# Attention scores of both maps as 64-row matmuls in the two halves of the array, three products each instead of four

## The chip, the cores and the metric

The kernel runs on one core of one Trainium2 chip. The metric is the device time of one execution in microseconds. Before the change the median of three runs is 3787.49 us (3784.84 to 3788.64).

## What is computed

One encoder block on 2048 tokens of 1024 channels: RMS norm, a projection, differential attention, a Hyena branch with long convolutions, the gated merge of both branches, and an expert-choice feed-forward layer with 16 experts. The change touches the differential attention alone: 4 heads, and for each head two softmax maps (m = 0 and 1) over queries and keys of 64 columns.

```python
def diff_attention(q, k, v, lam, subln_g, lambda_init):
    ...
    def block(qi):
        s = jnp.einsum('bhmqd,bhmkd->bhmqk', qi, k).astype(jnp.float32) * scale
        pr = jax.nn.softmax(s, axis=-1)
        a = pr[:, :, 0] - lam * pr[:, :, 1]
        return jnp.einsum('bhqk,bhkd->bhqd', a.astype(v.dtype), v)
    ...
```

## The kernel before

Numbers are carried as two parts, hi and lo, of 12 significant bits each, since the matmuls read the type float32r. A product a·b of two such numbers is taken as hi·hi + hi·lo + lo·hi (`mm3`, three matmuls, L48 to L50); the `split` of a tile is a copy on ACT (L42) and a subtraction on DVE (L43).

The program runs through five stages: the projection, the attention with pieces of the gate projection between its steps, the Hyena branch, the merge, and the experts. The change lies in `attn_phase` (L301). Its work is cut into 32 units, one for each head and each block of 256 queries. A unit has eight score steps, eight turns and eight steps of values:

- `prep_k` (L327) loads the keys of a head, splits them and transposes them, 512 tokens at a time, into the tile `k2`. The hi and the lo part of one map lie stacked in the 128 partitions: hi in partitions 0 to 63, lo in 64 to 127.
- `prep_q` (L355) does the same for the 256 queries of a unit, but writes each part twice: [hi; hi] and [lo; lo]. It takes 8 transposes (L367) and two copies on ACT (L368) a unit.
- `scores` (L388) is called eight times a unit. Each call takes one map, 128 queries and 1024 keys, in two pieces of 512 keys. A piece is two matmuls (L410) of 128 rows and 512 columns into one PSUM tile `p`: [hi; hi] and then [lo; lo] against [hi; lo] of the keys, which makes all four products. DVE then scales the piece into the tile `x` and takes its maximum (L411). After the second call of a map, ACT takes the exponentials of its 2048 columns (L418).
- `combine` (L420) puts the two maps of 128 queries together on DVE; `turn` (L429) transposes the result (L433) and splits it; `values` (L440) multiplies it with v (`mm3` into `pv`). The turns run 11 steps and the values 13 steps behind the scores.
- 150 pieces of `gate_steps` (L253), six matmuls of 512 columns into `gp` each, run between the steps.

The order in which the instructions stand on each engine is not that of the code: the tile framework schedules them when the kernel is built, and the engine then takes them in that order. Two pools that matter for it are these:

```python
        px = ctx.enter_context(pool_of(tc, name="at_s", bufs=6))
        ...
        ss = ctx.enter_context(pool_of(tc, name="at_ps", bufs=3, space=PSUM))
```

`at_ps` holds the PSUM tiles `p` of the scores, three of them, one bank each; `at_s` holds the tiles `x`.

Of the kernel before, what the change touches and what calls it, by code (L numbers as in the profile page):

```python
# [19 lines left out]
L = 2048  # L20
# [57 lines left out]
def rsqrt(nc, dst, tmp, src):  # L78
    """dst = src ** -0.5 with one Newton step after the activation table's root; src is kept."""
# [8 lines left out]
def rsqrt_mean(nc, dst, tmp, ss, n):  # L88
    """dst = (ss / n + EPS) ** -0.5; ss is overwritten."""
# [4 lines left out]
def proj_phase(E, x, norm1_g, w_in, conv_w, conv_b, qg, kg, rope, qn, kn, vs, hyc, ud, sg, mlp, gen):  # L94
    """u = RMSNorm(x); u @ w_in; q and k normed and turned, hy convolved; u turned, in two parts, to ud.
    The first 512 gate columns go to sg as gate_steps makes the others: they are last, token by token, for their
    u leaves its place to what follows.

    mlp and gen make generators of small pieces of other work, run between the products."""
    nc, tc = E.nc, E.tc  # L100
    with ExitStack() as ctx:
# [56 lines left out]
        def turned(c, w, t, pq):  # L158
            """q (c = 0) or k (c = 1): normed per 64 columns, with the rotation of the first 16."""
# [141 lines left out]
def attn_phase(E, qn, kn, vs, lams, subln_g, oT, filler, pieces):  # L301
    """Differential attention; oT [512 channels, tokens] gets the normed output.

    So many pieces of the filler run between its steps, for the vector engine holds the attention."""
    nc, tc = E.nc, E.tc
    QB = 256
    with ExitStack() as ctx:
# [19 lines left out]
        def prep_k(h, b):  # L327
            """k per map, [hi; lo] stacked along the contraction."""
            if b == 0:
                K2[h] = pk.tile([128, 2, L], F32R, name="k2")  # L330
            r = pr.tile([128, 4, 2, DK], F32, name="r")
            i = (nc.sync if h else nc.gpsimd).dma_start(r, dap(kn, b * 512 * 512 + h * 128, [[512, 128], [128 * 512, 4], [DK, 2],
                                                                                    [1, DK]]))
            if h == 0 and b == 1:
                E.second_k = i
            s = pr.tile([128, 4, 2, 2, DK], F32R, name="s")
            if h:
                split(nc, s[:, :, :, 0], s[:, :, :, 1], r)
            else:
                nc.vector.tensor_copy(s[:, :, :, 0], r)  # L340
                nc.vector.tensor_tensor(s[:, :, :, 1], r, s[:, :, :, 0].bitcast(F32), ALU.subtract)
            for m in range(2):
                p = sp.tile([128, 512], F32R, name="pp")
                for j in range(4):
                    nc.tensor.transpose(p[:, j * 128:(j + 1) * 128], s[:, j, m].rearrange("p a d -> p (a d)"), idr)
                nc.scalar.activation(K2[h][:, m, b * 512:(b + 1) * 512], p.bitcast(F32), AF.Copy)
# [8 lines left out]
        def prep_q(h, qb):  # L355
            """The queries of each map: [hi; hi] and [lo; lo] along the contraction."""
            r = pq.tile([128, 4, DK], F32, name="qr")
            nc.sync.dma_start(r.rearrange("p (t m) d -> p t (m d)", t=2),
                              dap(qn, qb * 256 * 512 + h * 128, [[512, 128], [128 * 512, 2], [1, 128]]))
            hl = pq.tile([128, 4, 2, 2, DK], F32R, name="qhl")  # L360
            r2 = r[:, :, None, :].to_broadcast([128, 4, 2, DK])
            split(nc, hl[:, :, 0], hl[:, :, 1], r2)
            qT = pq.tile([128, 4, 2, 128], F32R, name="qT")
            for a in range(2):
                p = sp.tile([128, 4, 128], F32R, name="pp")
                for tm in range(4):
                    nc.tensor.transpose(p[:, tm], hl[:, tm, a].rearrange("p a d -> p (a d)"), idr)  # L367
                nc.scalar.activation(qT[:, :, a], p.bitcast(F32), AF.Copy)  # L368
# [19 lines left out]
        def scores(u, c8):  # L388
            """One of eight steps: 1024 keys of one map for 128 queries; then the exponentials."""
            h, qb = units[u]  # L390
            t, m, c = c8 // 4, (c8 // 2) % 2, c8 % 2
# [8 lines left out]
            if m == 0 and c == 0:  # L400
                SM[u, t] = pq.tile([128, 12], F32, name="sm", bufs=6)
            sm = SM[u, t]
            if c == 0:
                EX[u, t, m] = px.tile([128, L], F32, name="x")
            x = EX[u, t, m]
            for i in range(2):
                o = c * 1024 + i * 512
                p = ss.tile([128, 512], F32, name="p")
                for a in range(2):
                    nc.tensor.matmul(p, qT[:, t * 2 + m, a], k2[:, m, o:o + 512], start=a == 0, stop=a == 1)  # L410
                nc.vector.tensor_scalar(x[:, o:o + 512], p, 0.125, None, ALU.mult, ALU.max,  # L411
                                        accum_out=sm[:, c * 2 + i:c * 2 + i + 1])
            if c == 0:
                return
            nc.vector.tensor_scalar(sm[:, 4:8], sm[:, 0:4], -1.0, None, ALU.mult, ALU.min,  # L415
                                    accum_out=sm[:, 8 + m:9 + m])
            acc = s0[:, qi:qi + 1] if m == 0 else sm[:, 10:11]
            nc.scalar.activation(x, x, AF.Exp, bias=sm[:, 8 + m:9 + m], accum_out=acc)  # L418
# [96 lines left out]
def hyena_tables():  # L515
    """Tables that hang on the shapes alone: positions, decay, and the pieces of a 4096-point DFT."""
# [33 lines left out]
    def parts(a):  # L550
        """The 12 significant bits that float32r carries, and the next 12."""
# [20 lines left out]
def filter_mlp(E, w, tabs, hsd):  # L572
    """The sine MLP on the positions; hsd gets the last layer as [hi; lo] along its channels.

    A generator: each step is a small piece of work, to run between another phase's."""
    nc, tc = E.nc, E.tc
    with pool_of(tc, name="fl_m", bufs=1, side="right") as pm, pool_of(tc, name="fl_ps", bufs=2, space=PSUM) as ps:
# [17 lines left out]
        def sine(p, out, layer):  # L595
            """out = sin(freq * (p + b)) with the argument brought into [-pi, pi] first."""
# [32 lines left out]
def filter_gen(E, w, tabs, hsd, filt):  # L629
    """filt [o, even/odd] (channel, t): sum and difference of the two sides of the filters, in steps."""  # L630
# [38 lines left out]
def hyena_phase(E, hyc, filt, skip, tabs, scr, hT, filler, then):  # L669
    """Two rounds of z <- gate * (conv(z) + skip * z) with 4096-point DFTs on the tensor engine.  # L670

    n = n2 + 128 n1 and k = k1 + 32 k2: first over n1 (16 of 32 are not zero), then, per k1, over n2 with the
    twiddles in the matrix; k1 from 0 to 16 is enough, since all sequences are real. What is left of
    the filler runs between the first steps; then(steps) runs the last steps between its own."""
    nc, tc = E.nc, E.tc
    vscr, z1 = scr["v"], scr["z1"]
    with pool_of(tc, name="hy_d", bufs=1) as pd, ExitStack() as right:
        with ExitStack() as ctx:
# [10 lines left out]
            def sums(v):  # L689
                """The factors of the sums over n1, with the imaginary ones negated for v = 1."""  # L690
# [32 lines left out]
            def parts_of(jobs):  # L723
                """The operands of the sums over n1, in their two parts: loads run ahead, and so does the split."""
# [28 lines left out]
            def first(it, v, side, busy=False):  # L753
                """B[n2, kr, c]: the sums over n1, in their two parts."""
# [17 lines left out]
            def dft_part(p, B, k, cr, ci):  # L772
                """cr times the real and ci times the imaginary sums over n1, over n2, for k1 = k."""
# [11 lines left out]
            def spectrum(it, s, side, busy=False):  # L785
                """The filter's spectrum: the real part (s = 0) and the imaginary one, negated (s = 1)."""
# [69 lines left out]
            def last(o, hf):  # L856
                """Back to n = n2 + 128 n1 with the sums over k1; then the skip and the gate."""
# [82 lines left out]
def merge_phase(E, x, sg, oT, hT, w_pa, w_ph, w_o, norm2_g, w_router, out, u2d, kept, steps):  # L940
    """x1 = x + (gates * branches) @ w_o to out, its norm to u2d, and the router's softmax into E.aff [128, tile, 16]
    of a pool that kept closes.

    steps: the last of the phase before, which makes hT; the first products of the attention branch run between."""
    nc, tc = E.nc, E.tc
    LEAD, AT = 3, (4, 10, 20, 26)
    with ExitStack() as ctx:
# [24 lines left out]
        def load(n, t):  # L972
            """The tile's branch and its gates."""
# [603 lines left out]
```

## Time and profile before

| what | before |
|---|---|
| median of 3 runs | 3787.49 us |
| lowest and highest run | 3784.84 and 3788.64 us |
| span of the profiled execution (its own time) | 3779.5 us |
| instructions in it | 58391 |
| PE busy | 3628.1 us, 96% of the span |
| DVE busy | 2399.3 us, 63% |
| ACT busy | 1739.1 us, 46% |
| mean granted TensorE clock | 0.980 |

The span is counted from the first to the last instruction; no time of that execution other than its span is shown, and the median of the runs is 8.0 us longer than it. In the rows below PE is the matmul part of TensorE and PEld its load of weights. A matmul's time in a row includes the tail in which its last columns leave the array, which lies beside the next matmul; the time that it takes from the engine is the distance from its start to the start of the next one.

### The profile page before, as it was taken

Reading aid. Unit: us, or ns where it says so; the run is one execution under the profiler, and the core shown is the slowest. Engines: PE = TensorE matmul, PEld = TensorE weight load, DVE = VectorE, ACT = ScalarE, POOL = GpSimd, SP = SyncE. Lnnn points to the kernel's source line nnn. Section 1 sums busy time; section 2 is a strip of 40 time slices with the busy share of each in tenths; the row PEclk is TensorE's granted clock in tenths of the full one; section 3 lists DMA queues with packets and bytes.
Section 4 is the critical chain, followed back from the end, with each engine's and each line's share of the span. In section 5 each row is a group of like instructions: output and inputs, shape, how many; then the busy total and the mean of one; then the engine's idle time right before and its main releaser. Section 6 shows DMA issues by size and latency. Waiting matters only on the chain. (4 is left out here: it accounts for less than half of the span.)

```text
span 3779.5 us, 58391 instructions
## 1 busy us (share of the span) xinstructions
PE 3628.1 (96%) x22727; PEld 3214.9 (85%) x22727; DVE 2399.3 (63%) x5111; ACT 1739.1 (46%) x2577; POOL 487.7 (13%) x436
## 2 busy tenths in 40 slices
PE   8999999999999999999999799995999999999998
PEld 6788888788888888799998588885889999999997
DVE  8944552698889897177778543447875555555553
ACT  5411111566666675367766433332344444444443
POOL 0000000000000000354454000003330101101000
PEclk9999999999999999999999799996999999999999
DMA  4286774323222232766776743333556666666664
GB/s 157 76 255 161 190 188 122 114 63 101 83 73 92 65 96 73 229 192 213 234 218 208 250 154 115 128 109 123 167 179 204 219 201 206 217 201 207 217 201 123
DMA packets 448681, 607.43 MB, mean 161 GB/s; under 512 B 36427, under 2 KB 332371, under 8 KB 441749
## 3 DMA queue, kind: packets, MB, share of 16 engines
q1 hardware_dynamic: 388261, 438.80, 36.7%
q0 software_dynamic: 34736, 127.16, 12.3%
q10 hardware_dynamic: 25408, 37.76, 2.8%
q8 instruction: 178, 2.92, 0.3%
q14 instruction: 98, 0.80, 0.1%
HBM read 464.16 MB, written 139.46 MB: 160 GB/s over the span
## 5 line engine op out<-in xcount | busy, mean ns | idle before, releaser
L43 DVE TENSOR_TENSOR wl<-r,wh 128x2048 fp32r<-128x2048 f32 (+1 forms) x232 | 440.7, 1904 | 336.4 <-ACT wh L42 336.1
L42 ACT ACTIVATE wh<-r 128x2048 fp32r<-128x2048 f32 (+1 forms) x232 | 372.1, 1605 | 567.4 <-issue 225.2
L48 PE MATMUL pg<-xh,wh 128*128 128x256 f32 x2048 | 584.4, 285 | 0.0
L49 PE MATMUL pg<-xl,wh 128*128 128x256 f32 x2048 | 581.2, 284 | 0.0
L50 PE MATMUL pg<-xh,wl 128*128 128x256 f32 x2048 | 581.0, 284 | 0.0
L48 PEld LDWEIGHTS pg<-xh,wh 128*128 128x128 f32 x2048 | 394.9, 193 | 5.9 <-ACT s L1461 5.3
L49 PEld LDWEIGHTS pg<-xl,wh 128*128 128x128 f32 x2048 | 394.9, 193 | 0.5
L50 PEld LDWEIGHTS pg<-xh,wl 128*128 128x128 f32 x2048 | 394.7, 193 | 0.0
L411 DVE TENSOR_SCALAR_CACHE_REDUCE x<-p 128x512 f32<-128x512 f32 x512 | 335.3, 686 | 25.0 <-PE p L410 24.2
L410 PE MATMUL p<-k,qT 128*128 128x512 f32 x1024 | 327.4, 415 | 0.0
L418 ACT ACTIVATE x<-x,sm 128x2048 f32<-128x2048 f32 x128 | 256.7, 2006 | 45.8 <-DVE sm L415 42.2
L42 ACT ACTIVATE ah<-pt 128x512 fp32r<-128x512 f32 x256 | 150.2, 595 | 153.4 <-PE pt L433 152.9
L48 PE MATMUL py<-wh,hh 128*128 128x512 f32 x512 | 205.0, 400 | 0.0
L48 PE MATMUL p<-wh,uh 128*128 128x512 f32 x512 | 203.6, 398 | 0.4 <-ACT uh L134 0.4
L49 PE MATMUL py<-wl,hh 128*128 128x512 f32 x512 | 202.8, 396 | 0.0
L50 PE MATMUL py<-wh,hl 128*128 128x512 f32 x512 | 202.8, 396 | 0.0
L50 PE MATMUL p<-wh,ul 128*128 128x512 f32 x512 | 200.4, 392 | 0.0
L49 PE MATMUL p<-wl,uh 128*128 128x512 f32 x512 | 200.3, 392 | 0.0
L43 DVE TENSOR_TENSOR al<-pt,ah 128x512 fp32r<-128x512 f32 x256 | 175.1, 686 | 38.6 <-ACT ah L42 37.3
L43 DVE TENSOR_TENSOR bl<-p,bh 128x512 fp32r<-128x512 f32 x192 | 124.8, 686 | 114.2 <-ACT bh L42 113.2
L410 PEld LDWEIGHTS p<-k,qT 128*128 128x128 f32 x1024 | 171.5, 190 | 24.5 <-ACT qT L368 2.8
L1484 POOL DMA_INDIRECT out_dram<-y,ix x32 | 68.5, 2141 | 778.8 <-ACT y L1483 672.2
(391 smaller groups left out, 9311.2 us busy)
## 6 DMA issues: line engine op xcount, KB each, us to landing
r<-in_w_gate SPq DMA_DIRECT2D x64, 1024.0 KB, 5.1
r<-in_w_up SPq DMA_DIRECT2D x64, 1024.0 KB
r<-in_w_down SPq DMA_DIRECT2D x64, 1024.0 KB, 5.8
gu<-s_ud POOLq DMA_DIRECT2D x48, 1024.0 KB, 5.9
tg<-in_tg POOLq DMA_DIRECT2D x68, 384.0 KB, 4.1
xt<-in_x SPq DMA_DIRECT2D x32, 512.0 KB, 6.5
s_filt<-fo SPq DMA_DIRECT2D x128, 128.0 KB, 3.2
zr<-s_filt SPq DMA_DIRECT2D x64, 256.0 KB, 2.7
```

The costliest lines, as they stand in the source:

```text
L42: nc.scalar.activation(hi, src, AF.Copy)
L43: nc.vector.tensor_tensor(lo, src, hi.bitcast(F32), ALU.subtract)
L48: nc.tensor.matmul(out, a[0], b[0], start=start, stop=False)
L49: nc.tensor.matmul(out, a[0], b[1], start=False, stop=False)
L50: return nc.tensor.matmul(out, a[1], b[0], start=False, stop=stop)
L410: nc.tensor.matmul(p, qT[:, t * 2 + m, a], k2[:, m, o:o + 512], start=a == 0, stop=a == 1)
L411: nc.vector.tensor_scalar(x[:, o:o + 512], p, 0.125, None, ALU.mult, ALU.max, accum_out=sm[:, c * 2 + i:c * 2 + i + 1])
L418: nc.scalar.activation(x, x, AF.Exp, bias=sm[:, 8 + m:9 + m], accum_out=acc)
L1484: nc.gpsimd.indirect_dma_start(out=rows, out_offset=bass.IndirectOffsetOnAxis(ap=ix[:, s:s + 1], axis=0), in_=y, in_offset=None, compute_o ...
```

## The change

The two maps' scores are made together. Instead of stacking hi and lo along the 128 rows, `k2` and `qT` now hold map 0 in partitions 0 to 63 and map 1 in partitions 64 to 127, and the hi and lo parts lie in tiles (index a or b) of their own. A score step takes both maps, 128 queries and 512 keys: six matmuls of 64 rows and 512 columns, hi·hi, hi·lo and lo·hi for each map, written so that map 0 (rows 0 to 63 of the array) and map 1 (rows 64 to 127) alternate. The fourth product, lo·lo, is left out, as in `mm3`. There are still 512 evictions of 512 columns; `prep_q` now takes 4 transposes and one copy on ACT a unit, and its split has 256 columns in place of 512. The exponentials of both maps are issued after the fourth step, one behind the other. The tile `sm` grows from 12 to 20 columns.

```diff
@@ prep_k
-            s = pr.tile([128, 4, 2, 2, DK], F32R, name="s")
+            s = pr.tile([128, 2, 4, 128], F32R, name="s")
...
-            for m in range(2):
+            for a in range(2):
                 p = sp.tile([128, 512], F32R, name="pp")
                 for j in range(4):
-                    nc.tensor.transpose(p[:, j * 128:(j + 1) * 128], s[:, j, m].rearrange("p a d -> p (a d)"), idr)
-                nc.scalar.activation(K2[h][:, m, b * 512:(b + 1) * 512], p.bitcast(F32), AF.Copy)
+                    nc.tensor.transpose(p[:, j * 128:(j + 1) * 128], s[:, a, j], idr)
+                nc.scalar.activation(K2[h][:, a, b * 512:(b + 1) * 512], p.bitcast(F32), AF.Copy)
@@ prep_q
-            r2 = r[:, :, None, :].to_broadcast([128, 4, 2, DK])
-            split(nc, hl[:, :, 0], hl[:, :, 1], r2)
-            qT = pq.tile([128, 4, 2, 128], F32R, name="qT")
+            split(nc, hl[:, 0], hl[:, 1], r)
+            qT = pq.tile([128, 2, 2, 128], F32R, name="qT")
+            p = sp.tile([128, 2, 2, 128], F32R, name="pp")
             for a in range(2):
-                p = sp.tile([128, 4, 128], F32R, name="pp")
-                for tm in range(4):
-                    nc.tensor.transpose(p[:, tm], hl[:, tm, a].rearrange("p a d -> p (a d)"), idr)
-                nc.scalar.activation(qT[:, :, a], p.bitcast(F32), AF.Copy)
+                for t in range(2):
+                    nc.tensor.transpose(p[:, a, t], hl[:, a, t], idr)
+            nc.scalar.activation(qT, p.bitcast(F32), AF.Copy)
@@ scores
-            t, m, c = c8 // 4, (c8 // 2) % 2, c8 % 2
+            t, c = c8 // 4, c8 % 4
...
-            if c == 0:
-                EX[u, t, m] = px.tile([128, L], F32, name="x")
-            x = EX[u, t, m]
-            for i in range(2):
-                o = c * 1024 + i * 512
-                p = ss.tile([128, 512], F32, name="p")
-                for a in range(2):
-                    nc.tensor.matmul(p, qT[:, t * 2 + m, a], k2[:, m, o:o + 512], start=a == 0, stop=a == 1)
-                nc.vector.tensor_scalar(x[:, o:o + 512], p, 0.125, None, ALU.mult, ALU.max,
-                                        accum_out=sm[:, c * 2 + i:c * 2 + i + 1])
-            if c == 0:
+            o = c * 512
+            ps = [ss.tile([128, 512], F32, name="p") for _ in range(2)]
+            for i, (a, b) in enumerate(((0, 0), (0, 1), (1, 0))):
+                for m in range(2):
+                    half = slice(m * DK, (m + 1) * DK)
+                    nc.tensor.matmul(ps[m], qT[half, a, t], k2[half, b, o:o + 512], start=i == 0, stop=i == 2)
+            for m in range(2):
+                nc.vector.tensor_scalar(EX[u, t, m][:, o:o + 512], ps[m], 0.125, None, ALU.mult, ALU.max,
+                                        accum_out=sm[:, 12 + m * 4 + c:13 + m * 4 + c])
+            if c < 3:
                 return
```

What the schedule makes of it on PE is seen at two places. In the rows, the number behind a name tells tiles of one name apart: of `p`, an odd and the next even number are not always a pair, but the two `p` of one score step are always the two numbers that follow each other in the list of all `p`, the first of map 0 and the second of map 1. "x3" at a row's end is three instructions that read alike. L409 and L435 of the changed kernel are L410 and L433 of the one before.

Before, on PE, in the middle of a unit: score pieces (L410), values (L48 to L50), turns (L433) and gate pieces.

```order
L433 MATMUL pt_6611<-idf_58,x_6197 128x128
L433 MATMUL pt_6611<-idf_58,x_6320 128x128
L433 MATMUL pt_6611<-idf_58,x_6197 128x128
L433 MATMUL pt_6611<-idf_58,x_6320 128x128
L410 MATMUL p_6620<-k2_5673,qT_6449 128x512 x2
L458 MATMUL pp_6607<-ones_5671,o2_6604 128x1 x2
L48 MATMUL pv_6630<-ah_6550,vh_5879 128x256
L49 MATMUL pv_6630<-al_6551,vh_5879 128x256
L50 MATMUL pv_6630<-ah_6550,vl_5880 128x256
L410 MATMUL p_6624<-k2_5673,qT_6449 128x512 x2
```

Each piece of 512 keys is a row of two matmuls that fill all 128 rows, and it does not matter what stands between two pieces.

With the change, on PE, one step (p_6655 and p_6656) in which the two maps alternate as written:

```order
L435 MATMUL pt_6646<-idf_58,x_6342 128x128
L409 MATMUL p_6655<-k2_5673,qT_6479 128x512
L409 MATMUL p_6656<-k2_5673,qT_6479 128x512
L409 MATMUL p_6655<-k2_5673,qT_6479 128x512
L409 MATMUL p_6656<-k2_5673,qT_6479 128x512
L409 MATMUL p_6655<-k2_5673,qT_6479 128x512
L409 MATMUL p_6656<-k2_5673,qT_6479 128x512
L435 MATMUL pt_6675<-idf_58,x_6211 128x128
```

The six matmuls stand between transposes of 128 rows. 113 of the 256 steps stand like this.

With the change, on PE, three steps of which the first still ends and the others begin (p_6521 is map 1 of one step, p_6548 and p_6549 are the two maps of the next, p_6582 and p_6583 those of the one after):

```order
L409 MATMUL p_6521<-k2_5673,qT_6479 128x512 x3
L409 MATMUL p_6548<-k2_5673,qT_6479 128x512 x3
L48 MATMUL pv_6395<-ah_6470,vh_5877 128x256
L49 MATMUL pv_6395<-al_6471,vh_5877 128x256
L50 MATMUL pv_6395<-ah_6470,vl_5878 128x256
L435 MATMUL pt_6573<-idf_58,x_6211 128x128
L435 MATMUL pt_6573<-idf_58,x_6342 128x128
L409 MATMUL p_6549<-k2_5673,qT_6479 128x512 x3
L435 MATMUL pt_6573<-idf_58,x_6211 128x128
L435 MATMUL pt_6573<-idf_58,x_6342 128x128
L409 MATMUL p_6582<-k2_5673,qT_6479 128x512 x3
```

Here the three products of a map stand behind one another, and those of the other map come only after values and transposes of 128 rows. In the whole order the 1536 score matmuls stand in 313 runs with other matmuls between them. Within the runs 445 matmuls of one map have one of the other map beside them that no other matmul has; 1536 - 445 = 1091 places are left, against 1024 matmuls before. 144 of the runs hold matmuls of one map alone.

## Rows read from the trace of the kernel before

**Rows 1.** The page: span, and busy time of each engine with its share.

```profile
span 3779.5 us, 58391 instructions
PE 3628.1 (96%) x22727; PEld 3214.9 (85%) x22727; DVE 2399.3 (63%) x5111; ACT 1739.1 (46%) x2577; POOL 487.7 (13%) x436
```

**Rows 2.** Stretches of the attention: us, busy by engine (instructions), clock, DMA share, GB/s.

```profile
800.00:900.00 100.00, 99.91 (x628) 86.83 (x627) 84.01 (x222) 64.64 (x98) 2.65 (x5) 1.00 0.22 68
...
sum 800.00, PE 796.45 PEld 691.40 DVE 707.93 ACT 530.86 POOL 19.66; mean PE 99.56 PEld 86.42 DVE 88.49 ACT 66.36 POOL 2.46
```

**Rows 3.** Groups by line, 700 to 1500 us: count | busy us, mean ns | idle before, releasers.

```profile
L411 DVE TENSOR_SCALAR_CACHE_REDUCE x<-p 128x512 f32<-128x512 f32 x512 | 335.3, 686 | 25.0 <-PE p L410 24.2
...
L418 ACT ACTIVATE x<-x,sm 128x2048 f32<-128x2048 f32 x128 | 256.7, 2006 | 45.8 <-DVE sm L415 42.2 <-DVE sm L424 3.2
...
L411 DVE DVE_READ_ACCUMULATOR x<-p 128x1 f32 x512 | 42.7, 83 | 0.0
```

**Rows 4.** Waits, 700 to 1500 us: who for whom, us, times, longest.

```profile
PEld p L410 <- ACT qT L368: 2.8, 12, 0.4
PEld p L410 <- DVE x L411: 1.2, 6, 0.3
```

**Rows 5.** Lines L410 and L455: duration ns min/median/max, first and last start us.

```profile
L410 PE MATMUL p<-k,qT x1024: 387/397/660, 697.5 to 1481.6; 128*128 128x512 f32 x171
...
L455 ACT ACTIVATE o<-pv x32: 371/378/390, 743.4 to 1508.4; 128x256 f32<-128x256 f32 x32
```

**Rows 6.** Timeline of PE in the attention: start us, us, what, count.

```profile
1051.44 0.28 PE L48 MATMUL pv<-ah,vh 128*128 128x256 f32 x1
1051.56 0.27 PE L49 MATMUL pv<-al,vh 128*128 128x256 f32 x1
...
1053.30 0.39 PE L49 MATMUL gp<-gl,gu 128*128 128x512 f32 x1
1053.53 0.39 PE L50 MATMUL gp<-gh,gu 128*128 128x512 f32 x1
1053.76 0.62 PE L410 MATMUL p<-k,qT 128*128 128x512 f32 x2
1054.22 0.40 PE L48 MATMUL gp<-gh,gu 128*128 128x512 f32 x1
```

**Rows 7.** Line L708, matmuls of 8 rows at the start of the Hyena stage.

```profile
L708 PEld LDWEIGHTS p<-sk,ex x2: 181/182/184, 1528.5 to 1528.6; 8*128 8x128 f32 x2
L708 PE MATMUL p<-sk,ex x2: 270/306/342, 1528.5 to 1528.7; 8*128 8x128 f32 x2
```

**Rows 8.** Timeline at L708, all engines.

```profile
1528.53 0.45 PE L708 MATMUL p<-sk,ex 8*128 8x128 f32 x2 [0.34 <-DMA sk<-in_hyena_skip]
1528.91 0.19 PEld L48 LDWEIGHTS gp<-gh,gu 128*128 128x128 f32 x1
1528.91 0.50 PE L48 MATMUL gp<-gh,gu 128*128 128x512 f32 x1
1529.02 0.19 PEld L49 LDWEIGHTS gp<-gl,gu 128*128 128x128 f32 x1
...
1529.24 0.39 PE L49 MATMUL gp<-gl,gu 128*128 128x512 f32 x1
1529.25 0.19 PEld L50 LDWEIGHTS gp<-gh,gu 128*128 128x128 f32 x1
```

**Rows 9.** Line L612, matmuls of 66 and of 128 rows in the projection stage.

```profile
L612 PE MATMUL fp<-emb,w x4: 590/591/592, 127.0 to 133.8; 66*128 66x512 f32 x4
...
L612 PE MATMUL fp<-h,w x4: 590/590/591, 139.7 to 146.4; 128*128 128x512 f32 x4
```

**Rows 10.** Timeline at L612, all engines.

```profile
127.03 1.02 PE L612 MATMUL fp<-emb,w 66*128 66x512 f32 x2
...
127.46 0.19 PEld L48 LDWEIGHTS p<-wh,uh 128*128 128x128 f32 x1 [0.24 <-PE p L50]
```

**Rows 11.** Timeline of PE at the transposes of a prep_q.

```profile
1055.99 0.54 PE L367 MATMUL pp<-idr,qhl 128*128 128x128 f32 x4
1056.36 0.35 PE L48 MATMUL pv<-ah,vh 128*128 128x256 f32 x1
```

More of the change, by code (lines that the diff above doesn't have):

```diff
@@ L330, in prep_k @@
                 K2[h] = pk.tile([128, 2, L], F32R, name="k2")
-            r = pr.tile([128, 4, 2, DK], F32, name="r")
-            i = (nc.sync if h else nc.gpsimd).dma_start(r, dap(kn, b * 512 * 512 + h * 128, [[512, 128], [128 * 512, 4], [DK, 2],
-                                                                                    [1, DK]]))
+            r = pr.tile([128, 4, 128], F32, name="r")
+            i = (nc.sync if h else nc.gpsimd).dma_start(r, dap(kn, b * 512 * 512 + h * 128,
+                                                               [[512, 128], [128 * 512, 4], [1, 128]]))
             if h == 0 and b == 1:
                 E.second_k = i
-            s = pr.tile([128, 4, 2, 2, DK], F32R, name="s")
+            s = pr.tile([128, 2, 4, 128], F32R, name="s")
             if h:
-                split(nc, s[:, :, :, 0], s[:, :, :, 1], r)
+                split(nc, s[:, 0], s[:, 1], r)
             else:
-                nc.vector.tensor_copy(s[:, :, :, 0], r)
-                nc.vector.tensor_tensor(s[:, :, :, 1], r, s[:, :, :, 0].bitcast(F32), ALU.subtract)
-            for m in range(2):
+                nc.vector.tensor_copy(s[:, 0], r)
+                nc.vector.tensor_tensor(s[:, 1], r, s[:, 0].bitcast(F32), ALU.subtract)
+            for a in range(2):
                 p = sp.tile([128, 512], F32R, name="pp")
                 for j in range(4):
-                    nc.tensor.transpose(p[:, j * 128:(j + 1) * 128], s[:, j, m].rearrange("p a d -> p (a d)"), idr)
-                nc.scalar.activation(K2[h][:, m, b * 512:(b + 1) * 512], p.bitcast(F32), AF.Copy)
+                    nc.tensor.transpose(p[:, j * 128:(j + 1) * 128], s[:, a, j], idr)
+                nc.scalar.activation(K2[h][:, a, b * 512:(b + 1) * 512], p.bitcast(F32), AF.Copy)
         def prep_v(h, b):
@@ L355, in prep_q @@
         def prep_q(h, qb):
[L357 to L360, printed above, removed]
-            r2 = r[:, :, None, :].to_broadcast([128, 4, 2, DK])
-            split(nc, hl[:, :, 0], hl[:, :, 1], r2)
-            qT = pq.tile([128, 4, 2, 128], F32R, name="qT")
+            r = pq.tile([128, 2, 128], F32, name="qr")
+            nc.sync.dma_start(r, dap(qn, qb * 256 * 512 + h * 128, [[512, 128], [128 * 512, 2], [1, 128]]))
+            hl = pq.tile([128, 2, 2, 128], F32R, name="qhl")
+            split(nc, hl[:, 0], hl[:, 1], r)
+            qT = pq.tile([128, 2, 2, 128], F32R, name="qT")
+            p = sp.tile([128, 2, 2, 128], F32R, name="pp")
             for a in range(2):
-                p = sp.tile([128, 4, 128], F32R, name="pp")
-                for tm in range(4):
-                    nc.tensor.transpose(p[:, tm], hl[:, tm, a].rearrange("p a d -> p (a d)"), idr)
-                nc.scalar.activation(qT[:, :, a], p.bitcast(F32), AF.Copy)
+                for t in range(2):
+                    nc.tensor.transpose(p[:, a, t], hl[:, a, t], idr)
+            nc.scalar.activation(qT, p.bitcast(F32), AF.Copy)
             return qT
@@ L399, in scores @@
             qT, s0 = QT[u], HS[h][1]
-            if m == 0 and c == 0:
-                SM[u, t] = pq.tile([128, 12], F32, name="sm", bufs=6)
+            if c == 0:
+                SM[u, t] = pq.tile([128, 20], F32, name="sm", bufs=6)
+                for m in range(2):
+                    EX[u, t, m] = px.tile([128, L], F32, name="x")
             sm = SM[u, t]
-            if c == 0:
-                EX[u, t, m] = px.tile([128, L], F32, name="x")
-            x = EX[u, t, m]
-            for i in range(2):
-                o = c * 1024 + i * 512
-                p = ss.tile([128, 512], F32, name="p")
-                for a in range(2):
-                    nc.tensor.matmul(p, qT[:, t * 2 + m, a], k2[:, m, o:o + 512], start=a == 0, stop=a == 1)
-                nc.vector.tensor_scalar(x[:, o:o + 512], p, 0.125, None, ALU.mult, ALU.max,
-                                        accum_out=sm[:, c * 2 + i:c * 2 + i + 1])
-            if c == 0:
-                return
[L415 to L418, printed above, removed]
+            o = c * 512
[4 more added lines that the diff above has]
+                    nc.tensor.matmul(ps[m], qT[half, a, t], k2[half, b, o:o + 512], start=i == 0, stop=i == 2)
+            for m in range(2):
+                nc.vector.tensor_scalar(EX[u, t, m][:, o:o + 512], ps[m], 0.125, None, ALU.mult, ALU.max,
+                                        accum_out=sm[:, 12 + m * 4 + c:13 + m * 4 + c])
+            if c < 3:
+                return
+            for m in range(2):
+                nc.vector.tensor_scalar(sm[:, m * 4:m * 4 + 4], sm[:, 12 + m * 4:16 + m * 4], -1.0, None, ALU.mult,
+                                        ALU.min, accum_out=sm[:, 8 + m:9 + m])
+                acc = s0[:, qi:qi + 1] if m == 0 else sm[:, 10:11]
+                x = EX[u, t, m]
+                nc.scalar.activation(x, x, AF.Exp, bias=sm[:, 8 + m:9 + m], accum_out=acc)
         def combine(u, t):
```

## The prediction

> **What bounds the kernel now.** I read the page first: TensorE's matmul part is busy for 3628.1 of 3779.5 us, 96%, and no other engine is over 63% but the weight loads that lie beside the matmuls [rows 1]. An average says little about one stage, so next come the stretches of the attention, which lasts from the first score matmul at 697.5 us to the squares of the last values at 1508.4 us [rows 5], 811 us. From 700 to 1500 us PE is busy 796.45 of 800 us, DVE 707.93 (88%), ACT 530.86, and the clock stands at 1.00 in the stretch printed, the upper of its two levels, 2.4 GHz [rows 2]. Then the waits: over the whole stage PE's weight loads for scores wait 1.2 us for a bank that DVE has to empty and 2.8 us for queries from ACT [rows 4]. So PE is never kept waiting: each 0.1 us that the change adds to or takes from a step on PE goes into the end, step by step, until DVE with its 88% becomes the bound.
>
> A busy row doesn't say what a matmul costs, because its tail lies beside the next one. The distance of starts does. Gate matmuls of 512 columns start at 1053.30 and 1053.53, the score matmul behind them at 1053.76, and the two scores there take until 1054.22: 0.23 us for 512 columns. Values of 256 columns start 0.12 us apart [rows 6]. I call 0.23 us a place.
>
> **The change, part by part.**
>
> *Places of the scores.* Before: 1024 matmuls [rows 5] at 0.23 us, 235.5 us. After: 1536 matmuls of 64 rows. Fewer rows don't shorten a matmul, its 512 columns still pass one by one: at L612 those of 66 rows last 591 ns and those of 128 rows 590 [rows 9]. So the gain must come from two halves working side by side. Had each matmul its partner, 768 places would remain and 256 x 0.23 = 58.9 us would be saved. But the schedule doesn't keep the alternation: only 445 matmuls have a partner beside them, and 1091 places remain. Even if two halves overlap fully, that is 67 x 0.23 = **15.4 us more**, not less. If they don't overlap at all, it is 512 x 0.23 = 117.8 us more. No row shows two matmuls in different halves, so both ends are kept; I take the full overlap, since the halves read different partitions and write different banks, and nothing in the rows makes them share anything but the sequence.
>
> *Switches of shape.* Between the 313 runs stand matmuls of 128 rows, so PE goes 313 times into the 64-row form and 313 times back. The trace has one return from a small form: the two matmuls of 8 rows at L708. The second one lasts 0.27 us [rows 7] and the pair ends at 1528.53 + 0.45 = 1528.98, so it began at 1528.71. It has 128 columns of type float32; such a matmul takes 0.43 us for 512 columns: at L612 the first of two starts at 127.03 and the second, which lasts 0.59 and ends at 128.05, at 127.46 [rows 9, 10]. So 128 columns are through at 1528.82. The next load, of a 128-row matmul, starts only at 1528.91, 0.09 later, and its matmul shows 0.50 instead of 0.39 us, 0.11 longer, for it waits for the load, which elsewhere runs beside the matmul ahead of it (1529.25 beside 1529.24) [rows 8]. One switch: 0.09 + 0.11 = 0.20 us. With 66 rows, which don't fit into half of the array, there is none of this: the load that follows starts at 127.46, together with the second matmul [rows 10]. These two rows are the ends, 0 and 0.20 us a switch. 64 rows fit into a part of the array as 8 do, so I take 0.20, for both directions: 626 x 0.20 = **125.2 us more**. Should the whole tail be waited for, 0.39 - 0.23 = 0.16, and the load behind it, a switch is 0.27 us.
>
> The Trainium skill states a rule here, in "TensorEngine Tiling (Array Packing)", Key Properties: changing the tiling mode, not merely the tile, drains TensorE. It speaks against this change, and names no price. By this rule, with the price of the 8-row return, the time is the forecast's, 3928 us; by the 66-row rows alone it would be rival B's, 3791 us. The trace agrees with the rule at the one place where it has such a change [rows 8].
>
> *The second half's load.* In a run that alternates, both halves need a fresh load before they start, and the loads stand 0.11 us apart (1528.91, 1529.02 [rows 8]), so the second half starts and ends 0.11 late. Passing through the 313 runs I count 105 in which this is at the end: 105 x 0.11 = **11.5 us more**. In the runs the loads themselves (0.11 each, two a place) fit into 0.23.
>
> *Queries.* `prep_q` loses 4 of its 8 transposes, 0.37 us for four [rows 11]; times 32 units that is **11.8 us less** on PE. The ACT copy and the half of DVE's split that go lie beside PE's work and count nothing. `prep_k` issues as much as before.
>
> *DVE, ACT and banks.* There are 512 evictions of 686 + 83 ns as before [rows 3], so DVE does 708 us or less in a stage that gets longer; it is no bound. Both exponentials of a step group come at its end and not one after two calls; the combine that needs them stands two steps behind, 2 x 811 / 256 = 6.3 us, and they take 2 x 2.0 [rows 3]. I cost this at nothing; without that cover DVE would wait, and after it the turns. The two matmul groups of a step need two of three banks at once. That is what the schedule answers with its runs of one map, and it is priced there; what is left of waiting for a bank on the chip is a rival.
>
> *Sum.* 15.4 + 125.2 + 11.5 - 11.8 = 140.3 us. The profiled execution spans 3779.5 us; it would be 3919.8. The median of the runs lies 8.0 us above that span, which I keep: 3787.5 + 140.3 = 3927.8, **3928 us**, 3.7% slower. Own range of this case: with 0.11 a switch (only the load is seen) 69 in place of 125, 3871; with 0.27 it is 169, 3971.
>
> **The rivals.**
>
> *A, the halves don't overlap.* Then 117.8 + 125.2 - 11.8 = 231.2 us more, 4019 us. For it: no row of this trace shows an overlap. Against: the operands are apart in rows and banks. The Trainium skill, "TensorE: Matmul & The Clock Gate", Part 3, gives 3.07 times the speed for four row tiles; no row here shows it, and by it the halves overlap mostly.
>
> *B, a switch between 64 and 128 rows is free*, as with 66 rows [rows 10]. Then only 15.4 - 11.8 = 3.6 us are added: 3791 us, not slower by what counts. The place is the start and end of each run, the price zero instead of 0.20, and it decides below (7.6 - 3.6) / 626 = 6 ns a switch. For it: the loads of 64-row matmuls could be pulled ahead like others. Against: [rows 8], where the load waited though nothing else held it.
>
> *C, the change does more than its order*: the halves run on by themselves, so that also runs of one map find their partner, and switches are free. 768 places, 58.9 + 11.8 = 70.7 us less, 3717 us; DVE's 708 us would still fit below the stage's length. Against: between separated runs stand 128-row matmuls that need both halves. The same Part 3 says that matmuls begin and end in program order, which would exclude it; nothing of it hangs in the sum.
>
> *D, PE waits for banks as well.* An eviction takes 0.77 us [rows 3]. If each of the 113 alternating steps waited for one, 87 us would come on top: 4015 us. For it: a pair takes two of three banks. Against: PE is slowed down and DVE isn't, and now PE waits 1.2 us in all [rows 4].
>
> **How the numbers follow.** Forecast 0.62, A 0.14, B 0.15, C 0.03, D 0.06. The time is that of the forecast, 3928. The range leaves out B and C, 0.18 together, and reaches from a little below 3871 to a little above 4019; for a switch that costs less than its load I open it down to 3830, and up to 4030. A measurement of this kernel can tell about 0.2%, 7.6 us. Faster by more than that: C, and a small part of B if the halves also shorten a place, 0.05. Within: most of B, 0.10. Slower: the forecast, A, D, 0.85.
>
> **What would show it.** In the profile after, the attention should last about 950 instead of 811 us, with PE as the bound and DVE nearer to 75% busy. In the timeline, a run of score matmuls should show its first load starting some 0.09 us after the last column of the 128-row matmul ahead of it, and the same behind its last; if those loads start together with the matmul ahead of them, the 125 us are wrong. Inside a run that alternates, matmuls of map 0 and map 1 should start about 0.11 apart and pairs 0.23; starts evenly 0.23 apart would be A. Waits of PE for DVE at L409 of many us would be D. A stage of unchanged length makes the prediction wrong.

## The result, and the profile after

The changed kernel takes 3915.11 us (median of 4 runs, 3910.63 to 3917.31), the kernel before 3786.16 us on the same chip (4 runs). The ratio is 1.0334, interval [1.0322, 1.0346]: 129.0 us slower. The forecast was 3928 us in a range of 3830 to 4030, with 140 us more.

From the page of the profile after, whose span is 3915.5 us:

```profile
PE 3753.3 (96%) x23111; PEld 3202.9 (82%) x23111; DVE 2397.3 (61%) x5111; ACT 1710.1 (44%) x2545; POOL 486.4 (12%) x436
```

PE's share is the 96% of [rows 1], and no other engine's rises: PE was the bound and is the bound, only for longer. An eviction on DVE takes 685 ns in the mean, against 686 [rows 3]. The line L457 (L455 before) and the score line, with first and last start:

```profile
L409 PE MATMUL p<-k,qT x1536: 383/393/503, 696.2 to 1607.0; 64*128 64x512 f32 x192
...
L457 ACT ACTIVATE o<-pv x32: 368/378/386, 754.1 to 1634.5; 128x256 f32<-128x256 f32 x32
```

From the first score to the last squares the attention now lasts from 696.2 to 1634.5, 938.3 us, against 697.5 to 1508.4, 810.9 us, in [rows 5]. So 127.4 of the 129 us lie in this stage. The stretches of 700 to 1600 us together:

```profile
sum 900.00, PE 890.98 PEld 652.51 DVE 691.80 ACT 490.10 POOL 18.51; mean PE 99.00 PEld 72.50 DVE 76.87 ACT 54.46 POOL 2.06
```

PE is still busy 99% of it; the share of DVE falls from 88 [rows 2] to 77%, since its work is the same and the stage longer. The weight loads fall from 86 to 72.5% though there are more of them: they stand idle at the switches, and two that lie side by side count once. The granted clock is 1.00 in each of these nine stretches. One step in which the maps alternate, in the timeline of PE and its loads (some rows are those of narrow windows, so that the first two matmuls, x2, can be told from all six, x6):

```profile
1101.83 0.60 PE L435 MATMUL pt<-idf,x 128*128 128x128 f32 x4
...
1102.15 0.27 PE L435 MATMUL pt<-idf,x 128*128 128x128 f32 x1
1102.35 0.19 PEld L409 LDWEIGHTS p<-k,qT 64*128 64x128 f32 x2 [0.17 <-DVE x L411]
1102.36 0.50 PE L409 MATMUL p<-k,qT 64*128 64x512 f32 x2
1102.36 0.97 PE L409 MATMUL p<-k,qT 64*128 64x512 f32 x6
...
1103.25 0.19 PEld L48 LDWEIGHTS gp<-gh,gu 128*128 128x128 f32 x1 [0.36 <-issue]
1103.25 0.50 PE L48 MATMUL gp<-gh,gu 128*128 128x512 f32 x1
```

Three things stand in it. First, the halves work side by side: two matmuls of 512 columns lie within 0.50 us, which is the length of one that waits for its load, and from the first load of the six to the load behind them it takes 0.90 us, three places and the price of one switch (six places alone would be 1.38). Second, the loads of the two halves lie side by side too: two of them take 0.19 us, the length of one. Third, the switches: the last of four transposes starts at 1102.15, the first at 1101.83, so they are 0.11 apart, and the last is through at about 1102.26; the first load of 64 rows starts at 1102.35, 0.09 later, and the matmul behind it lasts 0.50 where the usual length is 0.39. On the way back the load of the gate matmul starts 0.36 us after the last load before it ended, and its matmul again lasts 0.50. The chip does at 64 rows what it did at 8 rows [rows 8], and not what it did at 66 [rows 10].

### The profile page after: what moved, and what is told of

The parts are those of the page before. It is cut to its first block, busy times and chain, and to the rows that moved or that the text cites. A ratio compares the mean times of both kernels' runs of the same rounds, so it can differ in the third digit from the quotient of the medians.

```text
span 3915.5 us, 59106 instructions
## 1 busy us (share of the span) xinstructions
PE 3753.3 (96%) x23111; PEld 3202.9 (82%) x23111; DVE 2397.3 (61%) x5111; ACT 1710.1 (44%) x2545; POOL 486.4 (12%) x436
## 5 line engine op out<-in xcount | busy, mean ns | idle before, releaser
L48 PE MATMUL pg<-xh,wh 128*128 128x256 f32 x2048 | 584.9, 286 | 0.0
L50 PE MATMUL pg<-xh,wl 128*128 128x256 f32 x2048 | 581.5, 284 | 0.0
L48 PEld LDWEIGHTS pg<-xh,wh 128*128 128x128 f32 x2048 | 395.3, 193 | 5.9 <-ACT s L1463 5.3
L50 PEld LDWEIGHTS pg<-xh,wl 128*128 128x128 f32 x2048 | 395.2, 193 | 0.0
L409 PE MATMUL p<-k,qT 64*128 64x512 f32 x1536 | 343.0, 427 | 5.7 <-ACT qT L366 3.5
L409 PEld LDWEIGHTS p<-k,qT 64*128 64x128 f32 x1536 | 182.0, 184 | 95.4 <-issue 30.6
L43 DVE TENSOR_TENSOR al<-pt,ah 128x512 fp32r<-128x512 f32 x256 | 174.8, 686 | 54.3 <-ACT ah L42 53.7
L48 PE MATMUL py<-wh,hh 128*128 128x512 f32 x512 | 205.1, 401 | 0.0
L48 PE MATMUL p<-wh,uh 128*128 128x512 f32 x512 | 203.5, 398 | 0.4 <-ACT uh L134 0.4
L50 PE MATMUL py<-wh,hl 128*128 128x512 f32 x512 | 203.1, 397 | 0.0
L50 PE MATMUL p<-wh,ul 128*128 128x512 f32 x512 | 200.4, 392 | 0.0
L48 PE MATMUL gp<-gh,gu 128*128 128x512 f32 x384 | 166.7, 434 | 3.7 <-ACT go L294 3.5
```

Of the source, the lines that this page charges most:

```text
L409: nc.tensor.matmul(ps[m], qT[half, a, t], k2[half, b, o:o + 512], start=i == 0, stop=i == 2)
```

## The experiments

Differences are to the kernel before, run on the same chip beside each of them (3781 to 3783 us).

**serial64: the same products, map by map.**

```diff
-            for i, (a, b) in enumerate(((0, 0), (0, 1), (1, 0))):
-                for m in range(2):
+            for m in range(2):
+                for i, (a, b) in enumerate(((0, 0), (0, 1), (1, 0))):
```

> The three products of map 0 are written ahead of those of map 1, so that the halves seldom stand side by side: by the order on PE 299 runs and 1310 places (only the last matmul of one map and the first of the next overlap) against 313 and 1091 in the changed kernel. Theory (halves overlap, a switch of shape costs about 0.21 us): 3915 + 219 x 0.23 - 28 x 0.21 = about 3959 us. Rival A (halves don't overlap): the number of matmuls is the same, so 3915 less 6, 3909 us. Rival B (switches free, the loss is elsewhere): also about 3965, so this run tells only A from the rest.

Measured 3908.74 us, ratio 1.0337 [1.0319, 1.0354]: 127.9 us more, as the changed kernel, where the theory had 173 (3959 against 3786): 45 us less. The order on PE is as expected: all of its 133 runs of six have three products of one map ahead of three of the other. The trace shows why that costs nothing. In 89 of them the six end as three pairs, not more than a tenth of a place apart. One of these, PE and its loads:

```profile
1065.26 0.19 PEld L409 LDWEIGHTS p<-k,qT 64*128 64x128 f32 x2 [0.17 <-issue]
1065.26 0.50 PE L409 MATMUL p<-k,qT 64*128 64x512 f32 x2
...
1066.16 0.19 PEld L48 LDWEIGHTS pv<-ah,vh 128*128 128x128 f32 x1 [0.36 <-issue]
```

Two matmuls start together again, and from the first load to the load behind the run it takes 0.90 us, exactly as in the alternating run above (1102.35 to 1103.25). So the step of the theory that fell is that matmuls of two halves start in the order in which they are written. The rows don't name the map, but six products take three places here, so the two that start together must be of different halves: the second half's first product starts beside the first half's first, though all three products of that half are written ahead of it. The time of this run doesn't tell whether halves overlap; the starts in the traces do, and rival A falls by them.

**serial128: that order, without a switch and without halves.** The edit, shown against serial64, leaves out the selection of rows, so each score is the sum over both maps.

```diff
-                    half = slice(m * DK, (m + 1) * DK)
-                    nc.tensor.matmul(ps[m], qT[half, a, t], k2[half, b, o:o + 512], start=i == 0, stop=i == 2)
+                    nc.tensor.matmul(ps[m], qT[:, a, t], k2[:, b, o:o + 512], start=i == 0, stop=i == 2)
```

> The same order on PE as serial64 (299 runs), but each score matmul reads all 128 rows, so that there is no switch of shape and no overlap; the scores are the sum over both maps, the output is not the reference's. Theory: 1536 places instead of 1024 and no switch, 3786 + 512 x 0.23 - 13 (fewer transposes of queries) = about 3891 us, faster than serial64 by 68 us though it has 226 places more. Rival B (switches free): slower than serial64 by 226 x 0.23 = 52 us. Rival D (waits for banks and queries make the loss): the same bank pattern, so about as slow as the changed kernel or slower, 3915 to 3970 us.

Measured 3889.41 us, ratio 1.0291 [1.0273, 1.0308]: 108.5 us more, where the theory had 105. It has the 299 runs of serial64, with no shape to change, and is 19 us faster than it, although none of its matmuls share a place. In serial64's trace 402 matmuls end within 0.06 us of another, so 1134 places are left; serial128 has 402 more, 92 us at 0.23. So 598 switches cost 92 + 19 = 111 us: 0.19 us each, an estimate, since matmuls that overlap in part are not counted as sharing. The granted clock is alike, 0.998 in both from the first to the last score matmul.

The two traces also give the price without counting places, for one and the same run of three products between gate matmuls, first in serial64 and then in serial128:

```profile
747.44 0.40 PE L50 MATMUL gp<-gh,gu 128*128 128x512 f32 x1
...
748.99 0.39 PE L49 MATMUL gp<-gl,gu 128*128 128x512 f32 x1
```

```profile
745.55 0.39 PE L50 MATMUL gp<-gh,gu 128*128 128x512 f32 x1
...
746.68 0.39 PE L49 MATMUL gp<-gl,gu 128*128 128x512 f32 x1
```

From the start of the matmul ahead of the run to that of the second one behind it, it takes 1.55 us with two switches and 1.13 without. (The run starts at 747.77 and the matmul behind it at 748.65; without switches these are 745.78 and 746.46.) Over the 112 runs of three products, all at a granted clock of 1.00, the median difference is 0.40 us: **0.20 us a switch**. serial128 bounds one part of rival D as well: PE's loads for scores wait 0.6 us for banks in it. Halves that work side by side fill the same three banks faster; what that does is seen in hp3 below.

**dose64 and dose128: switches added.** Both add one small matmul of zeros to each step of the changed kernel; it changes no value. In dose64 it has the form of its neighbours, in dose128 all 128 rows.

```diff
+                if i == 0:
+                    nc.tensor.matmul(ps[0][:, :8], zr[:DK], zr[:DK, :8], start=False, stop=False)   # dose64
+                    nc.tensor.matmul(ps[0][:, :8], zr[:], zr[:, :8], start=False, stop=False)       # dose128
```

> The changed kernel with one matmul more in each of the 256 steps, after the first product of each map: zeros of 64 rows, 8 columns, added onto map 0's scores, which changes no value. It has the form of its neighbours, so no switch is added: by the order on PE 618 switches, against 626 in the changed kernel. Every theory: the changed kernel's +129 us and the small matmul, at most 256 x 0.06 = 15 us: 3910 to 3930 us beside a kernel before of 3783.

> The same, but the added matmul of zeros has 128 rows, so that each step is cut in two: by the order 1130 switches, 512 more than in dose64, and nothing else is different. Theory (a switch of shape costs about 0.21 us of PE): 512 x 0.21 = 107 us more than dose64, some 4020 to 4040 us, and a few us more where the cut keeps a half from running ahead. Rival (switches are nearly free, the loss is waits for banks and queries): within 20 us of dose64.

Measured: dose64 3927.41 us, ratio 1.0382 [1.0364, 1.0399]; dose128 4024.73 us, ratio 1.0634 [1.0616, 1.0652]. The difference is 97.3 us between the two medians for 512 switches, 0.190 us each. One cut step of dose128, PE:

```profile
1062.67 0.50 PE L413 MATMUL p<-k,qT 64*128 64x512 f32 x2
1063.10 0.27 PE L415 MATMUL p<-zr 128*128 128x8 f32 x1
1063.30 0.73 PE L413 MATMUL p<-k,qT 64*128 64x512 f32 x4
1063.96 0.50 PE L49 MATMUL gp<-gl,gu 128*128 128x512 f32 x1
```

A matmul of 8 columns, whose own columns pass in a few ns (0.23 us for 512), pushes the next products 0.20 us behind its own start, and the step takes 1.29 us where the uncut one above takes 0.90: 0.39 us for two switches.

The division by 512 is not clean, though, for the two kernels differ in two more ways. First, the granted clock: from the first to the last score matmul it is 1.00 in dose64 and 0.96 in dose128. The stretch from 1500 to 1600 us in each, dose64 first (us, busy by engine, clock, DMA share, GB/s):

```profile
1500.00:1600.00 100.00, 98.98 (x569) 72.20 (x568) 76.50 (x197) 49.86 (x76) 2.06 (x4) 1.00 0.18 56
1500.00:1600.00 100.00, 100.00 (x488) 70.21 (x489) 67.00 (x176) 47.35 (x70) 1.59 (x3) 0.90 0.20 66
```

That alone is about 0.037 x 1030 = 38 us of dose128, an estimate; all four runs of dose128 have a lower mean clock (0.971 to 0.975) than those of dose64 (0.980 to 0.981). Second, the small matmul of 64 rows isn't free: where the clock is 1.00, a run of six takes 0.90 us in the changed kernel, 1.01 with it and 1.30 with that of 128 rows (medians of 127, 134 and 127 runs). Between the two kernels that is 0.29 us a step, 74 us for 256 of them, and with the clock 112 us; why 97 were measured stays open. Against the uncut step it is 0.41 us, 0.20 a switch. That the division by 512 comes out at 0.190 is in part luck. What stands is that the form of the matmul costs and not the interruption alone: dose64 interrupts as often and adds 0.12 us to a step, not 0.41.

**hppair, quad and hp3: fewer switches.** Three ways of keeping a step in one run. In hp3 the six matmuls stand in the scheduler's highest priority; hppair also gives both maps one tile of two banks; quad makes two steps at once in one tile of four.

```diff
+            with tc.high_priority():                                       # all three
-        ss = ctx.enter_context(pool_of(tc, name="at_ps", bufs=3, space=PSUM))
-        st = ctx.enter_context(pool_of(tc, name="at_pt", bufs=2, space=PSUM))
+        ss = ctx.enter_context(pool_of(tc, name="at_ps", bufs=2, space=PSUM))   # hppair; 1 in quad
+        st = ctx.enter_context(pool_of(tc, name="at_pt", bufs=1, space=PSUM))   # hppair and quad
-            ps = [ss.tile([128, 512], F32, name="p") for _ in range(2)]
+            pb = ss.tile([128, 2, 512], F32, name="p")                           # hppair; [128, 2, 2, 512] in quad
```

> Both maps' banks are one tile of two banks, two of them (four banks in all, the turns have one bank instead of two), and the six matmuls have the scheduler's highest priority: by the order on PE 162 runs that hold one or two whole steps, 768 places. Theory: 3786 - 256 x 0.23 + 324 x 0.21 - 13 = about 3782 us, no difference from before, and if the single bank of the turns costs something, a little over it. Rival D (banks): each step needs a whole tile to be empty, so waits of PE for DVE grow, 3830 us or more. Rival A (no overlap): 3786 + 118 + 68 - 13 = 3959 us.

> Two steps, 1024 keys of both maps, share one tile of four banks (a single one; the turns have one bank) and stand in one run of twelve matmuls with the scheduler's highest priority: 128 runs, 768 places. Theory: 3786 - 59 + 256 x 0.21 - 13 = about 3768 us, 0.5% faster than before, if PE finds other work while DVE empties the four banks (3.1 us of DVE a run, 4 us of other PE work a run). Rival D (banks): each run waits for the end of the evictions of the run before, 1 us or more x 128, 3890 us or more. Rival B (switches free): 3714 us.

> The changed kernel with one edit: its score matmuls have the scheduler's highest priority, so that other matmuls seldom come between; banks as in the changed kernel (three and two). By the order on PE 143 runs instead of 313, and if a run takes as many places as its fuller half has matmuls, 900 places. Theory (0.21 us a switch, halves independent): 3781 - 124 x 0.23 + 286 x 0.21 - 13 = about 3800 us; waits for the three banks inside long runs come on top, up to some 60 us. Rival (the switches are not the cost, but the waits for banks): 3900 us or more, as the changed kernel.

Measured: hppair 3856.32 us, ratio 1.0203 [1.0186, 1.022]; quad 3898.96, ratio 1.0315 [1.0297, 1.0332]; hp3 3887.88, ratio 1.0271 [1.0254, 1.0288]. All three lie under the changed kernel's ratio, quad by little, and none comes near the kernel before. The waits of the stage in hppair (engine, line, for whom: us, times, longest):

```profile
PEld p L411 <- DVE x L413: 57.0, 136, 0.8
PEld pt L437 <- DVE al L43: 48.7, 101, 1.2
```

A load that waits at a switch shows about 0.17 us of it in such rows, and up to 0.37 behind a gate piece, so of hppair's 57.0 us at the scores 136 x 0.17 = 23 or more are switches and the rest, at most 34 us, are banks that DVE has not emptied; 28 us of waits lie inside its runs, where there is no switch. The other row is the single bank of the turns. In quad PE hardly waits for score banks (1.6 us) but for the split turns (54.3 us), for the norms' operands (36.8) and for the bank of the turns (34.2), and its clock from the first to the last score matmul is 0.986. That shows where it waits; which cut would free it stays open. Its 128 runs of twelve show the overlap best: they take 1.59 us in the median, where twelve places would be 2.8.

In hp3 only 166 matmuls end within 0.06 us of another, though the scores stand in 143 runs. Its long runs go at the pace of DVE, which empties one bank after another; from the middle of a run of 21:

```profile
751.03 0.68 DVE L412 TENSOR_SCALAR_CACHE_REDUCE x<-p 128x512 f32<-128x512 f32 x1
751.64 0.68 DVE L412 TENSOR_SCALAR_CACHE_REDUCE x<-p 128x512 f32<-128x512 f32 x1
```

The evictions start 0.61 us apart, and runs of 15, 18 and 21 products take 3.26, 3.87 and 4.47 us (medians): 0.61 us more for each bank of three products, where two halves side by side would need 0.69 us for two banks. So a longer run alone saves switches here but not places: 313 matmuls inside the runs had to wait for their load (they last 0.47 us or more), and 270 of them start 0.04 to 0.08 us after an eviction has ended.

**before4: the banks divided as in hppair, on the kernel before.**

```diff
-        ss = ctx.enter_context(pool_of(tc, name="at_ps", bufs=3, space=PSUM))
-        st = ctx.enter_context(pool_of(tc, name="at_pt", bufs=2, space=PSUM))
+        ss = ctx.enter_context(pool_of(tc, name="at_ps", bufs=4, space=PSUM))
+        st = ctx.enter_context(pool_of(tc, name="at_pt", bufs=1, space=PSUM))
```

> The kernel before with the banks divided as in hppair and quad: four for the scores, one instead of two for the turns. Nothing else is changed. Theory W1 (the single bank of the turns is what hppair lacks to its 3782 us): slower than before by some 50 to 75 us, about 3840 us, with waits of PE at the turns for DVE and ACT. Theory W2 (the whole tile of two banks that has to be empty is what costs): no difference, 3781 us within 10.

Measured 3816.78 us, ratio 1.0088 [1.0072, 1.0104]: 33.6 us more, between the two theories and part of both. So hppair's 75 us are, by estimate, about 34 for the turns' bank (if it costs there what it costs here) and 28 to 34 of waits for score banks; places and switches by themselves nearly balance: -211 x 0.23 + 324 x 0.20 - 13 = 3 us, with the 813 places of its trace.

**qonly and qearly: the one part of the change that saves.** The scores stay as before; the queries are split and transposed once, as in the change, and ACT writes them to both halves of the partitions. qearly also makes them three steps earlier.

```diff
...
-                for tm in range(4):
-                    nc.tensor.transpose(p[:, tm], hl[:, tm, a].rearrange("p a d -> p (a d)"), idr)
-                nc.scalar.activation(qT[:, :, a], p.bitcast(F32), AF.Copy)
+                for t in range(2):
+                    nc.tensor.transpose(p[:, a, t], hl[:, a, t * 2:t * 2 + 2].rearrange("p m d -> p (m d)"), idr)
+            for m in range(2):
+                src = p[m * DK:(m + 1) * DK].rearrange("p a t c -> p t a c").bitcast(F32)
+                for s in range(2):
+                    nc.scalar.activation(qT.rearrange("p (t m) a c -> p m t a c", m=2)[s * DK:(s + 1) * DK, m], src, AF.Copy)
@@ scores, qearly alone
...
+            if u == 0 and c8 == 0:
+                QT[u] = prep_q(h, qb)
+            if c8 == 5 and u + 1 < len(units):
+                QT[u + 1] = prep_q(*units[u + 1])
             if c8 == 0:
-                QT[u] = prep_q(h, qb)
```

> The kernel before, scores as before, but the queries are split and transposed once (4 transposes a unit instead of 8, a split of 256 columns instead of 512) and ACT writes the result four times, 64 partitions each, instead of twice. Theory: PE is the bound and loses 128 transposes of 0.09 us, 12 us less, 3769 us. Rival: ACT's two more copies a unit (64 more of about 0.4 us) are late, since PE waits for the queries in 12 cases already, no gain or some us more.

> As qonly, but the queries of the next unit are made at the sixth score step of the unit ahead instead of at its own first. Theory: qonly took 14 us of transposes off PE and got 8 of them back in waits for ACT's copies; with the copies three steps earlier the waits go, and about 10 us of the 12 show: 3773 us, 0.3% faster than before. Rival: PE has as many waits elsewhere since ACT does more, no difference from before (within 0.1%).

Measured: qonly 3781.82 us, ratio 0.9998 [0.9989, 1.0007], no difference; qearly 3773.27 us, ratio 0.9979 [0.997, 0.9988], 0.2% faster than the kernel before. PE's loads for scores wait 12.6 us for queries in qonly (27 times), 0.4 us in qearly (once) and 2.8 us in [rows 4]. qonly took 12 us of transposes off PE and turned most of them into waits for ACT; with the queries made earlier the waits are gone and 10 us of the 12 show.

## Why the prediction was right

The forecast's mechanism held, and the main term of its sum too; a term of 11.5 us had no ground. Without it the sum is 128.8 us against 129.0 measured, but that nearness is chance: the places cost some 8 us more than was counted, and the terms as the traces show them add up to some 8 us more than was measured.

- **PE bounds the stage, and time on PE goes into the end**: shown. 127.4 of 129 us lie in the attention, PE is busy 99% there, DVE went to 77%, where the prediction had 75.
- **Places of the scores, 15.4 us**: 411 of 1536 matmuls end within 0.06 us of the one before in the trace, so 1125 places, 23.2 us more than 1024. The prediction counted 1091, from the order, with halves that keep their order. They don't (serial64), which gives the runs written map by map a share too; but a map's bank is not always free in time, and then the halves run one after the other: 78 matmuls inside the runs had to wait for their load, and all of them start 0.04 to 0.08 us after an eviction has ended. Both were left out, and they nearly balance. What mattered was right: the schedule's order and not the code's tells how many matmuls find a partner, and it ate the 59 us that full pairing would have given.
- **Switches, 125.2 us at 0.20**: shown by serial64 against serial128, run by run (0.20), and by the cut step of dose128 against the uncut one (0.20); their whole times give 0.19, less cleanly. So the term stands: 626 x 0.20 = 125 us, 119 at 0.19. With the places as measured the sum is 23.2 + 125.2 - 11.8 = 137 us, 8 more than was measured (130 at 0.19). About 3 of the 8 are clock: the granted clock is 0.996 from the first to the last score matmul of the kernel before and 1.000 in the changed one. The rest stays open. The choice between the two nearest rows was the prediction's main choice, and the 8-row return was the right one: 0.09 after the last column, 0.11 for the load. The drain that the Trainium skill states in "TensorEngine Tiling (Array Packing)", Key Properties, is seen here at 64 rows, with that price. The return costs what the entry costs: in the run of three above the matmul ahead and the first one behind each stand 0.10 to 0.11 us further from the next, and the run itself takes 0.20 us longer.
- **The second half's load, 11.5 us**: wrong, it is nothing. The distance of 0.11 us between loads in [rows 8] is that of loads into one and the same place; loads into two halves lie side by side (1102.35, two in 0.19 us).
- **Queries, 11.8 us less**: the right size; qearly shows 10 of it by itself.
- **DVE and ACT at no cost**: PE's loads at L409 wait 22.3 us for DVE and 13.0 for ACT, of which 0.17 us or more in each of 77 and 29 cases are the switch; at most some 9 and 8 us are left, against 1.2 and 2.8 before [rows 4].

```profile
PEld p L409 <- DVE x L411: 22.3, 77, 0.6
```

Of the rivals, A falls by the starts in the trace, B by the run of three and the cut step, C because its switches would have to be free, though its idea that a half runs on by itself turned out true inside a run. D is there, but as waits with at most some 13 us and not 87; its larger part hides in the places, where a bank that isn't free takes a pair apart. An eviction takes 0.61 us of DVE where they stand back to back (hp3); the 0.77 that the prediction added up are two rows that overlap.

## What to carry to other kernels

Two halves of the array take two 64-row matmuls in one place, but each change between them and matmuls of 128 rows costs 0.20 us here; count how often the schedule goes in and out, and set that against the 0.23 us that a pair of 512 columns saves. Here a step saves one place, 0.23, and pays two switches, 0.40, even where its run stays whole; two steps to a run would come out a little ahead, 0.46 against 0.40, if nothing else waited, which it did (hppair, quad). Longer runs then meet the next bound, DVE with 0.61 us a bank (hp3). Before a matmul is packed tighter, read the built order, not the loop: a pool that is short by one bank can take the pairs apart again. And before two kernels are subtracted to get the price of one instruction, compare their granted clocks (dose128).

## What was not expected of the hardware

- Matmuls in the two halves don't start in program order. In serial64 the fourth of six starts beside the first (1065.26, two in 0.50 us). "TensorE: Matmul & The Clock Gate" of the Trainium skill states in Part 3 that matmuls start and end in program order; for two row halves with banks of their own this trace shows otherwise.
- Weight loads of the two halves run side by side: two in 0.19 us where two loads for one place take 0.11 more (1102.35 against 1529.02 in [rows 8]).
- The small matmul of 64 rows in dose64 cost more than its columns: 3927.4 - 3915.1, with the kernels before at 3782.4 and 3786.2, is 16 us for 256 of them, 0.06 us each. In its runs of six it is 0.12 us; where half of that comes back is not shown.
- In dose128, the slowest of these kernels, the granted clock fell below 1.00 in five of the ten stretches of 100 us from 700 to 1700 us, to 0.90 in two, though PE is busy 99 to 100% in each; in dose64 it is 1.00 in the nine from 700 to 1600. What brings it down is not shown.
